# A gated pooling and forgetting-attention block: the transposes of V written to the score banks instead of the projection banks

## Chip, cores, metric

The kernel runs on one core of one Trainium2 chip. The metric is the device time of one execution in microseconds (us). Five engines work side by side, each through its own instructions in order: PE (TensorE, matmuls and transposes), ACT (ScalarE), DVE (VectorE), POOL (GpSimd) and SP (SyncE, which here issues transfers). They wait for one another by semaphores. PE's results go to PSUM, which this kernel uses as 8 banks of 128 x 512 fp32; a bank can be written again once everything in it has been read out ("evacuated") by ACT and DVE.

## What is computed

One decoder block on 1040 tokens (16 meta tokens, 1024 real ones) of width 1024. The part that matters here, cut from the reference:

```python
h = rmsnorm(x, norm_g)
proj = jnp.einsum('bld,dn->bln', h, w_in)
u_pool, z_pool, q, k, v, z_attn, f_logit, g_pool, g_attn = jnp.split(proj, _split_points(), axis=-1)
y_pool = causal_multiscale_pool(u_pool, pool_w, pool_scale) * jax.nn.silu(z_pool)
log_f = jax.nn.log_sigmoid((f_logit + b_forget).astype(jnp.float32))
y_attn = forgetting_attention(q, k, v, log_f).reshape(B, L, ATTN_WIDTH) * jax.nn.silu(z_attn)
merged = (jax.nn.sigmoid(g_pool) * jnp.einsum('blc,cd->bld', y_pool, w_up_pool)
          + jax.nn.sigmoid(g_attn) * jnp.einsum('blc,cd->bld', y_attn, w_up_attn))
return x + jnp.einsum('bld,de->ble', merged, w_out)
# in the attention, 8 heads of 64, causal, c = cumulative sum of log_f:
s = q @ k.T / 8 + c[query] - c[key];  o = softmax(s) @ v
```

## The kernel before

**Stages.** The norm, the transposes of the input and the projections of the first two heads come first (to about 55 us), then the attention (to about 466 us), then the gates, the up-projections and the output projection. Every product is done in fp32 precision by splitting operands into a high and a low part and adding three products (`g_mm3`): 24 matmuls per projection piece.

**Attention.** The 8 heads go in 4 pairs `p`. Each pair has 4 units (head `e` of the pair, half of the queries); the 16 units run one after the other. For a unit `qk` computes scores of one block of 128 keys against up to 512 queries (two matmuls, L691 and L692), ACT and DVE evacuate them (L696, L700). `soft` does the exponentials (L732 to L737) and `av` multiplies by V (L753). While unit i does `soft` and `av`, the scores of unit i+1 are computed.

**Filling.** PE's order is written out by the program, not by a scheduler. Between the attention's matmuls a queue (`Fill`, called through `F.pull`) hands out matmuls of the other projections in a set amount of PE time. Among them are `f_q`, `f_k` and `f_v` of the next pair: q, k and v of two heads. The orders of ACT, DVE and POOL come from a scheduler.

**V.** `f_v(p)` projects V with the channels on the partitions, in three pieces of 384, 384 and 272 tokens (`PIECES`). ACT copies each piece to `vt` in SBUF (L301). The attention needs V with the keys on the partitions, so `v_blocks` transposes `vt` in blocks of 128 keys on PE (L312) and ACT and DVE split the result into high and low part (L321, L322), for the two heads one after the other. After the second piece blocks 1 and 2 are transposed, after the third 3 to 5, and after another projection blocks 6 to 8 and 0. Pair 0 has its blocks 6 to 8 and 0 directly ahead of the first scores (L802).

**Banks.** In the attention the 8 PSUM banks are shared out so: `pj` two, for the projection pieces; `psS` two and `pk` one, which form a ring of three for the scores; `psT` two (running maxima and others); `psO` one (the output of `av`). The ring is turned by `third`: every third call gives the `pk` bank, which also carries the name `pj`, so in this kernel's profile a score in `pj` lies in the third bank of the ring. A projection piece takes a bank by `fill_bank`, which in the attention (`spare[0]` false) gives the two `pj` banks in turn; before the attention (`spare[0]` true) it turns through `pj` and `pk`.

Of the kernel before, what the change touches and what calls it, by code (L numbers as in the profile page):

```python
# [45 lines left out]
def r32(ap):  # L46
    return ap.bitcast(F32)
# [7 lines left out]
def tile_hybrid_block(ctx, tc, x, meta, norm_g, w_in, b_forget, pool_w, pool_scale,  # L55
# [118 lines left out]
    turn, spare = [0], [True]  # L174

    def third(pool, name):
        turn[0] += 1
        if turn[0] % 3 == 0:
            return pk.tile([128, 512], F32, name="pj")
        return pool.tile([128, 512], F32, name=name)  # L180

    def fill_bank():
        return third(pj, "pj") if spare[0] else pj.tile([128, 512], F32, name="pj")
# [121 lines left out]
            V[p, e] = ap_.tile([KB, NB, 2, 64], F32R, name="V", bufs=3)  # L305

    def v_blocks(p, *parts):
        pt = fill_bank().rearrange("p (n e d) -> p n e d", e=2, d=64)
        n = 0
        for b0, b1 in parts:  # L310
            for b in range(b0, b1):
                nc.tensor.transpose(pt[:, n], VT[p][:, KS[b]:KS[b] + KB], ident)  # L312
                n += 1
                yield 109.0
        for e in range(2):
            n = 0
            for b0, b1 in parts:
                pv = pt[:, n:n + b1 - b0]
                n += b1 - b0
                vh = V[p, e][:, b0:b1, e, :]  # L320
                nc.scalar.activation(vh, pv[:, :, e, :], AF.Copy)  # L321
                nc.vector.tensor_tensor(V[p, e][:, b0:b1, 1 - e, :], pv[:, :, e, :], r32(vh), op=ALU.subtract)  # L322
# [13 lines left out]
    def f_v(p):  # L336
        w = w_chunk(COL_V + p * 128)
        VT[p] = gp.tile([128, L], F32, name="vt", tag="g")
        v_alloc(p)
        for c0, c1 in PIECES:  # L340
            yield from v_piece(p, w, c0, c1)
            if c0:
                yield from v_blocks(p, {384: (1, 3), 768: (3, 6)}[c0])
# [135 lines left out]
    for n, (kind, t0, t1) in enumerate(todo):  # L479
# [29 lines left out]
        if n in (4, 7, 10):  # L509
            run(v_blocks(0, (max(1, 2 * (n // 3) - 2), 2 * (n // 3))))  # L510
    G_.close()
    spare[0] = False
    psS = P_.enter_context(tc.tile_pool(name="psS", bufs=2, space=PS, reuse_waits="tile"))
# [279 lines left out]
    def pair_fill(p):  # L793
        if p < 4:
            F.add(f"q{p}", f_q(p))
            F.add(f"k{p}", f_k(p), apart=True)
            F.add(f"v{p}", f_v(p), 4 * p - 2)
            F.add(f"v{p}", v_blocks(p, (6, 9), (0, 1)), 4 * p - 2, apart=True)
# [506 lines left out]
    for n in range(7):  # L1305
        if n < 6:
            prep(n + 1)
        ps = ba if n in (0, 2, 4, 6) else bb_
# [56 lines left out]
```

## Time and profile before

| what | value |
|---|---|
| three runs | 731.11, 730.85, 730.51 us; median 730.85 |
| profiled execution | 731.65 us, of which the span from first to last instruction 730.0 us |
| granted TensorE clock | 0.998 |
| PE busy | 714.1 us of the span |
| stalls of PE in the attention, 100 to 470 us | 5.8 us in four groups |

The profile is of one execution. `PE` rows are matmuls and transposes, `PEld` their weight loads, which run beside them. In a row of the timeline the first number is the start in us from the span's start, the second the time until the last of the row's instructions ended; `x4` is their count, and the bracket is the engine's idle time ahead of them and what ended it. Matmuls are pipelined: the end of one lies behind the start of the next, so what an instruction costs is read from start to start. In a row of the waits stand the total in us, the number of times and the longest. A stall of PE costs time only if nothing later would have waited anyway.

### The profile page before, as it was taken

The page shows a single profiled execution, that of the slowest core. Times are in us where ns is not written, and L with a number is a line of the kernel's source. Part 1 is how long each engine was busy: PE and PEld are TensorE (multiplying, and loading weights), DVE is VectorE, ACT ScalarE, POOL GpSimd, SP SyncE. Part 2 cuts the span into 40 slices and gives each one's busy share as a digit, 9 for nine tenths or more (in the row PEclk, how much of TensorE's full clock was granted, in tenths as well). Part 3 has the DMA queues.
Part 4 walks back from the last instruction along what each step waited for, and adds up shares of the span by engine and source line. Part 5 has one row for each costly group of instructions (what it writes and reads, how often), then busy time and mean ns, then how long its engine had stood idle before and what let it go on. Part 6 is the DMA issues. An engine that isn't in the chain of part 4 may idle for free.

```text
span 730.0 us, 10821 instructions
## 1 busy us (share of the span) xinstructions
PE 714.1 (98%) x3637; PEld 614.1 (84%) x3637; DVE 506.5 (69%) x913; ACT 425.0 (58%) x930; POOL 329.6 (45%) x409
## 2 busy tenths in 40 slices
PE   8999999999999989999999999999999999999996
PEld 6997999988889878789888888888888888888885
DVE  5743487676688766877876768765877654888775
ACT  6652577566686666667765577252766423525445
POOL 5412236638455574363643775493743010006142
PEclk9999999999999999999999999999999999999999
DMA  9201124772987558729556789486905367671006
GB/s 303 65 27 33 58 58 161 184 251 75 284 208 182 128 147 215 210 62 273 116 115 176 238 219 214 125 314 196 321 9 213 106 215 260 230 259 59 0 1 230
DMA packets 88505, 119.39 MB, mean 164 GB/s; under 512 B 11297, under 2 KB 54305, under 8 KB 86450
## 3 DMA queue, kind: packets, MB, share of 16 engines
q1 hardware_dynamic: 84896, 99.83, 42.4%
q0 software_dynamic: 2256, 16.25, 12.5%
q10 hardware_dynamic: 1298, 2.63, 1.0%
q8 instruction: 28, 0.46, 0.3%
q14 instruction: 27, 0.22, 0.1%
HBM read 92.81 MB, written 53.67 MB: 201 GB/s over the span
## 4 chain that ended last, share of the span: by engine, by line
PE 84%; ACT 5%; DVE 4%; issue 1%; POOL 0%; POOLq 0%; DVEq 0%; ACTq 0%
PE pj L171 52%; PE pj L1245 8%; PE pj L986 8%; PE po L753 5%; PE pt L986 3%; PE pt L1245 2%; PE ps L692 2%; PE ps L691 2%; ACT S L733 1%; PE pj L528 1%; PE pj L692 1%; PE pj L691 1%; ACT qa L269 1%; ACT ph L736 1%; DVE ql L273 0%
## 5 line engine op out<-in xcount | busy, mean ns | idle before, releaser
L171 PE MATMUL pj<-hh,whi 128*128 128x512 f32 (+3 forms) x640 | 146.0, 354 | 6.5 <-ACT vt L301 4.4
L171 PE MATMUL pj<-hh,wlo 128*128 128x512 f32 (+3 forms) x640 | 143.2, 350 | 0.3 <-POOL wlo L446 0.3
L171 PE MATMUL pj<-hl,whi 128*128 128x512 f32 (+3 forms) x640 | 141.5, 350 | 0.0
L171 PEld LDWEIGHTS pj<-hh,whi 128*128 128x128 f32 x640 | 107.7, 188 | 21.8 <-ACT vt L301 5.8
L159 POOL TENSOR_TENSOR wlo<-raw,whi 128x256 fp32r<-128x256 f32 x116 | 88.9, 809 | 79.2 <-ACT whi L157 26.9
L171 PEld LDWEIGHTS pj<-hl,whi 128*128 128x128 f32 x640 | 108.1, 188 | 12.0
L171 PEld LDWEIGHTS pj<-hh,wlo 128*128 128x128 f32 x640 | 107.9, 188 | 11.9 <-POOL wlo L446 0.5
L737 DVE TENSOR_TENSOR pl<-S,ph 128x512 fp32r<-128x512 f32 (+4 forms) x112 | 82.3, 743 | 25.7 <-ACT ph L736 24.6
L745 POOL TENSOR_TENSOR acc<-acc,S 128x272 f32<-128x272 f32 (+4 forms) x80 | 74.5, 931 | 13.8 <-ACT S L733 8.8
L705 DVE TENSOR_TENSOR pt<-pt,S 128x400 f32<-128x400 f32 (+2 forms) x96 | 46.6, 486 | 22.3 <-ACT S L696 20.1
L736 ACT ACTIVATE ph<-S 128x512 fp32r<-128x512 f32 (+4 forms) x112 | 52.9, 481 | 15.1 <-PE po L753 14.3
L137 POOL TENSOR_TENSOR gw<-graw,gw 128x256 fp32r<-128x256 f32 x40 | 45.8, 1180 | 29.6 <-ACT gw L966 13.1
L733 ACT ACTIVATE S<-S 128x512 f32<-128x512 f32 (+4 forms) x112 | 49.7, 478 | 10.8 <-DVE S L732 10.5
L732 DVE TENSOR_TENSOR S<-S,pt 128x512 f32<-128x512 f32 (+4 forms) x112 | 50.7, 497 | 0.7
L696 ACT ACTIVATE S<-ps,negc 128x512 f32<-128x512 f32 (+4 forms) x63 | 32.4, 518 | 20.8 <-PE ps L692 16.7
L986 PE MATMUL pj<-gh,gw 128*128 128x512 f32 x180 | 42.0, 389 | 0.0
L1138 DVE TENSOR_TENSOR rl<-pj,rl 128x512 f32<-128x512 f32 x32 | 22.0, 689 | 28.6 <-PE pj L171 28.2
L157 ACT ACTIVATE whi<-raw 128x512 fp32r<-128x512 f32 x58 | 34.4, 623 | 12.5 <-DMA raw<-in_w_in_dram 6.9
L986 PEld LDWEIGHTS pj<-gh,gw 128*128 128x128 f32 x180 | 33.8, 188 | 7.1
L743 POOL TENSOR_TENSOR acc<-S 128x400 f32<-128x400 f32 (+1 forms) x16 | 19.7, 1231 | 40.8 <-ACT S L733 40.8
L753 PE MATMUL po<-pl,V 128*128 128x512 f32 (+4 forms) x112 | 37.4, 334 | 0.0
L1245 PE MATMUL pj<-opw 128*128 128x512 f32 (+1 forms) x168 | 36.2, 374 | 0.0
(236 smaller groups left out, 1339.3 us busy)
## 6 DMA issues: line engine op xcount, KB each, us to landing
raw<-in_w_in_dram SPq DMA_DIRECT2D x31, 512.0 KB, 4.4
gs<-in_w_in_dram SPq DMA_DIRECT2D x5, 1024.0 KB, 10.0
td<-in_w_out_dram SPq DMA_DIRECT2D x5, 1024.0 KB, 8.2
xt<-in_x_dram SPq DMA_DIRECT2D x8, 512.0 KB, 7.5
sp_gp<-st SPq DMA_DIRECT2D x16, 256.0 KB, 4.1
gs<-gs POOLq DMA_DIRECT2D x4, 1024.0 KB, 9.0
td<-td POOLq DMA_DIRECT2D x4, 1024.0 KB, 9.2
sp_ga<-st SPq DMA_DIRECT2D x16, 256.0 KB, 5.2
```

What stands on the lines that cost most here:

```text
L137: ins = nc.gpsimd.tensor_tensor(out[:, c:c + 256], x[:, c:c + 256], y[:, c:c + 256], op=op)
L159: ins = nc.gpsimd.tensor_tensor(lo[:, k:k + 2], raw[:, k:k + 2], r32(hi[:, k:k + 2]), op=ALU.subtract)
L171: nc.tensor.matmul(ps, a, b, start=(i == 0), stop=(i == len(seq) - 1))
L705: nc.vector.tensor_tensor(m[:kb, c0:], m[:kb, c0:], s[:kb, c0:], op=ALU.max)
L732: nc.vector.tensor_tensor(s[:kb, c0:], s[:kb, c0:], self.pm[:kb, c0:], op=ALU.subtract)
L733: exps.append(nc.scalar.activation(s[:kb, c0:], s[:kb, c0:], AF.Exp))
L736: nc.scalar.activation(ph[:kb, c0:], s[:kb, c0:], AF.Copy)
L737: dves.append(nc.vector.tensor_tensor(pl[:kb, c0:], s[:kb, c0:], r32(ph[:kb, c0:]), op=ALU.subtract))
L745: accs.append(nc.gpsimd.tensor_tensor(acc[:kb, c0:], acc[:kb, c0:], s[:kb, c0:], op=ALU.add))
L753: nc.tensor.matmul(self.po[:, c0:], v, r[:kb, c0:], start=(b == 0 and i == 0), stop=(b == self.nb - 1 and i == 1))
L986: nc.tensor.matmul(ps, op_w[n][p][k // 2][:, k % 2, i * 128:(i + 1) * 128], op_h[n][q][k // 2][:, k % 2], start=start and m == 0, stop=m = ...
L1245: nc.tensor.matmul(ps, pick(A_, k, p)[:, i * 128:(i + 1) * 128], pick(B_, k, q)[:, c0:c1], start=start and n == 0, stop=n == 11, skip_grou ...
```

## The change

The transposes of V in the attention take their bank from the ring of the scores (`third(psS, "ps")`) instead of from the two `pj` banks. Before the attention nothing changes.

```diff
     def v_blocks(p, *parts):
-        pt = fill_bank().rearrange("p (n e d) -> p n e d", e=2, d=64)
+        pt = (fill_bank() if spare[0] else third(psS, "ps")).rearrange("p (n e d) -> p n e d", e=2, d=64)
```

Ten calls of `v_blocks` lie in the attention: one of pair 0, three each of pairs 1, 2 and 3. No instruction comes or goes, and PE and SP keep their order; each call turns the ring by one, so the later scores lie in other banks of it, and the projection pieces alternate between their two banks without the transposes in between.

First place, PE in `f_v(1)`: the end of the second piece (`pj_1904`), the transposes of blocks 1 and 2 (`pj_1969`), and the first matmuls of the third piece (`pj_1976`). Before:

```order
L171 MATMUL pj_1904<-hh1_124,wlo_1833 128x384 x4
L312 MATMUL pj_1969<-ident_96,vt_1840 128x128 [waits Activation_49]
L312 MATMUL pj_1969<-ident_96,vt_1840 128x128
L171 MATMUL pj_1976<-hh0_122,whi_1832 128x272 [waits Activation_49]
L171 MATMUL pj_1976<-hh0_122,whi_1832 128x272 x3
```

The same place with the change:

```order
L171 MATMUL pj_1904<-hh1_124,wlo_1833 128x384 x4
L312 MATMUL pj_1969<-ident_96,vt_1840 128x128 [waits DVE_49]
L312 MATMUL pj_1969<-ident_96,vt_1840 128x128
L171 MATMUL pj_1976<-hh0_122,whi_1832 128x272 x4
L171 MATMUL pj_1976<-hh1_124,whi_1832 128x272
```

The third piece had the bank of the second and waited for ACT, which copies the second piece to `vt`; now it has the bank of the first and carries no wait, and the transposes (here in the `pk` bank, hence still `pj`) wait for DVE, which reads an earlier score.

Second place, PE a little later: the end of the third piece, the transposes of blocks 3 to 5 (2028), and the first matmuls of the next projection (`pj_2047`). Before:

```order
L171 MATMUL pj_1976<-hh1_124,wlo_1833 128x272 x4
L312 MATMUL pj_2028<-ident_96,vt_1840 128x128 [waits DVE_49,PE_49]
L312 MATMUL pj_2028<-ident_96,vt_1840 128x128 x2
L171 MATMUL pj_2047<-hh0_122,whi_2038 128x512 [waits PE_49,Activation_49]
L171 MATMUL pj_2047<-hh0_122,whi_2038 128x512 x3
```

With the change:

```order
L171 MATMUL pj_1976<-hh1_124,wlo_1833 128x272 x4
L312 MATMUL ps_2028<-ident_96,vt_1840 128x128 [waits DVE_49,Activation_49]
L312 MATMUL ps_2028<-ident_96,vt_1840 128x128 x2
L171 MATMUL pj_2047<-hh0_122,whi_2038 128x512 x4
L171 MATMUL pj_2047<-hh1_124,whi_2038 128x512 x4
```

Here too the projection behind the transposes loses its wait.

Third place, PE at the first unit: the transposes of pair 0 (1040) and the first five scores, of 512, 400, 272, 144 and 16 queries, among matmuls of a projection. Before:

```order
L312 MATMUL pj_1040<-ident_96,vt_283 128x128 x3
L691 MATMUL ps_1055<-qa_228,ka_160 128x512
L692 MATMUL ps_1055<-ql_229,ka_160 128x512
L171 MATMUL pj_1064<-hh0_122,whi_965 128x272 [waits Activation_49]
L171 MATMUL pj_1064<-hh0_122,whi_965 128x272 x3
L691 MATMUL ps_1069<-qa_228,ka_160 128x400
L692 MATMUL ps_1069<-ql_229,ka_160 128x400
L171 MATMUL pj_1064<-hh1_124,whi_965 128x272 x4
L691 MATMUL pj_1080<-qa_228,ka_160 128x272
L692 MATMUL pj_1080<-ql_229,ka_160 128x272
L171 MATMUL pj_1064<-hl0_123,whi_965 128x272 x4
L691 MATMUL ps_1090<-qa_228,ka_160 128x144 [waits DVE_49]
```

With the change:

```order
L312 MATMUL ps_1040<-ident_96,vt_283 128x128 x4
L691 MATMUL ps_1055<-qa_228,ka_160 128x512
L692 MATMUL ps_1055<-ql_229,ka_160 128x512
L171 MATMUL pj_1064<-hh0_122,whi_965 128x272 [waits Activation_49]
L171 MATMUL pj_1064<-hh0_122,whi_965 128x272 x3
L691 MATMUL pj_1069<-qa_228,ka_160 128x400
L692 MATMUL pj_1069<-ql_229,ka_160 128x400
L171 MATMUL pj_1064<-hh1_124,whi_965 128x272 x4
L691 MATMUL ps_1080<-qa_228,ka_160 128x272 [waits DVE_49]
L692 MATMUL ps_1080<-ql_229,ka_160 128x272
L171 MATMUL pj_1064<-hl0_123,whi_965 128x272 x4
L691 MATMUL ps_1090<-qa_228,ka_160 128x144 [waits DVE_49]
```

By the built program's memory map the third score (1080) now lies in the bank of the first (1055), and the fourth (1090) in the bank of the transposes (1040); before, the third had the `pk` bank and the fourth the bank of the first. So the fourth score now waits for the last of the eight instructions that evacuate the transposes.

On ACT, DVE and POOL the scheduler moves a few rows by a few places near 93, 162, 264 and 357 us: exponentials, evacuations of keys and V, and some of the weight splits (L157, L159).

## Prediction

> **What bounds the kernel now.** I read the page first: the busy shares and the chain that ended last.
>
> ```profile
> PE 714.1 (98%) x3637; PEld 614.1 (84%) x3637; DVE 506.5 (69%) x913; ACT 425.0 (58%) x930; POOL 329.6 (45%) x409
> PE 84%; ACT 5%; DVE 4%; issue 1%; POOL 0%; POOLq 0%; DVEq 0%; ACTq 0%
> ```
>
> PE is busy for 714.1 of 730.0 us and carries 84% of the chain; no other engine comes near. What ends the kernel sooner must take away PE's idle time, some 16 us in all, or PE's work, which this change leaves as it is. So the next view is the busy time by stretches, to see where the idle time of the attention lies.
>
> ```profile
> 180.00:275.00 95.00, 92.75 (x476) 80.88 (x475) 70.84 (x146) 64.41 (x160) 53.80 (x66) 1.00 0.73 190
> 370.00:466.00 96.00, 95.93 (x451) 80.28 (x450) 72.10 (x137) 59.25 (x142) 58.58 (x68) 1.00 0.74 192
> 466.00:600.00 134.00, 134.00 (x592) 110.66 (x590) 91.11 (x97) 66.72 (x88) 54.44 (x51) 1.00 0.59 194
> ```
>
> The first column behind the length is PE. Where pair 2 of V is prepared (180 to 275) it idles 2.25 us; after the last preparation (370 to 466), with the same attention work, 0.07 us, and from 466 to 600 nothing. The attention's chain through DVE and ACT therefore does not hold PE up. What does is in the waits of PE from 100 to 470 us:
>
> ```profile
> PE pj L171 <- ACT vt L301: 4.4, 6, 1.0
> PE pj L171 <- ACT qa L269: 0.8, 1, 0.8
> PE pj L171 <- DVE ka L296: 0.4, 1, 0.4
> PE pj L171 <- ACT st L354: 0.2, 1, 0.2
> ```
>
> Projections (L171) wait for the evacuation of an earlier projection. Six of the waits, 4.4 us, are for the copy of V into `vt`: two in each of three pairs. No row has `po`: the multiplication by V never waits for the softmax, nor do the scores for their banks.
>
> **The nine waits that go.** In the attention a projection's transposes take one `pj` bank, so the projection behind them gets the bank of the projection just ahead of them, whose copy has hardly begun. With the change the projections alternate among themselves, and each finds a bank whose copy was started a whole piece earlier. The timeline of PE shows the nine places, each as the transposes and the first matmuls behind:
>
> ```profile
> 157.36 0.38 PE L312 MATMUL pj<-ident,vt 128*128 128x128 f32 x2
> 158.70 0.89 PE L171 MATMUL pj<-hh,whi 128*128 128x272 f32 x5 [0.96 <-ACT vt L301]
> ...
> 162.06 0.49 PE L312 MATMUL pj<-ident,vt 128*128 128x128 f32 x3
> 162.77 2.14 PE L171 MATMUL pj<-hh,whi 128*128 128x512 f32 x8 [0.22 <-ACT vt L301]
> ...
> 176.81 0.60 PE L312 MATMUL pj<-ident,vt 128*128 128x128 f32 x4
> 177.66 0.50 PE L171 MATMUL pj<-hh,whi 128*128 128x512 f32 x1 [0.25 <-ACT st L354]
> ...
> 258.91 0.38 PE L312 MATMUL pj<-ident,vt 128*128 128x128 f32 x2
> 260.20 1.14 PE L171 MATMUL pj<-hh,whi 128*128 128x272 f32 x7 [0.91 <-ACT vt L301]
> ...
> 264.23 0.49 PE L312 MATMUL pj<-ident,vt 128*128 128x128 f32 x3
> 265.69 1.20 PE L171 MATMUL pj<-hh,whi 128*128 128x512 f32 x4 [0.96 <-ACT vt L301]
> ...
> 280.72 0.66 PE L312 MATMUL pj<-ident,vt 128*128 128x128 f32 x4
> 281.44 2.12 PE L171 MATMUL pj<-hh,whi 128*128 128x512 f32 x8
> ...
> 350.01 0.38 PE L312 MATMUL pj<-ident,vt 128*128 128x128 f32 x2
> 350.96 1.27 PE L171 MATMUL pj<-hh,whi 128*128 128x272 f32 x8 [0.57 <-ACT vt L301]
> ...
> 354.07 0.49 PE L312 MATMUL pj<-ident,vt 128*128 128x128 f32 x3
> 355.29 2.11 PE L171 MATMUL pj<-hh,whi 128*128 128x512 f32 x8 [0.72 <-ACT vt L301]
> ...
> 369.77 0.60 PE L312 MATMUL pj<-ident,vt 128*128 128x128 f32 x4
> 370.13 0.31 PE L691 MATMUL ps<-qa,ka 128*128 128x144 f32 x1
> 370.28 0.28 PE L692 MATMUL ps<-ql,ka 128*128 128x144 f32 x1
> 370.62 0.50 PE L171 MATMUL pj<-hh,whi 128*128 128x512 f32 x1
> ```
>
> The bracket understates the loss, since the pipeline also runs empty while the last transposes end. From start to start it is the whole distance less what unhindered transposes take. Four take 0.36 us (369.77 to 370.13, where a score follows at once); two take 0.14 us, by a place ahead of the attention:
>
> ```profile
> 42.70 0.38 PE L312 MATMUL pj<-ident,vt 128*128 128x128 f32 x2
> 42.84 0.36 PE L171 MATMUL pj<-hh,whi 128*128 128x256 f32 x1
> ```
>
> Three I put between, at 0.25 us. Pair 1 loses 1.34 - 0.14 = 1.20, 0.71 - 0.25 = 0.46 and 0.85 - 0.36 = 0.49; pair 2 loses 1.15, 1.21 and 0.36; pair 3 loses 0.81, 0.97 and, behind the 144-wide score at 370.28 that takes some 0.11 us, 0.23. Together 6.9 us. The least is what the waits list names, 4.4 + 0.2 = 4.6 us. I take 6.9, since 370 to 466 shows that PE without such waits runs without gaps.
>
> Does it stay gained? Behind each place PE's next waits must hold too. The transposes themselves now wait for a score's evacuation; the score tile of three turns ago was written several us earlier, and its readers are done long before (no score waits for a bank in the list above). The remaining chain moves along: the softmax of a unit starts with PE's own scores.
>
> **The wait that comes.** Pair 0's transposes are directly followed by the five scores of the first unit with little other work between, and the fourth score stands behind the evacuation of the transposes. Rows of PE, then of DVE:
>
> ```profile
> 85.69 0.29 PE L691 MATMUL pj<-qa,ka 128*128 128x272 f32 x1
> ...
> 86.44 0.23 PE L691 MATMUL ps<-qa,ka 128*128 128x144 f32 x1
> 86.50 0.28 PE L692 MATMUL ps<-ql,ka 128*128 128x144 f32 x1
> 86.61 0.33 PE L171 MATMUL pj<-hl,whi 128*128 128x272 f32 x1
> ...
> 85.16 0.34 DVE L700 SCALAR_TENSOR_TENSOR S<-ps,negc,mask 128x112 f32<-128x112 f32 x1 [0.39 <-ACT S L696]
> 87.11 0.21 DVE L322 TENSOR_TENSOR V<-pj,V 128x64 fp32r<-128x64 f32 x1
> ```
>
> The last evacuation ended at 87.32 us; the order of ACT and DVE up to it is unchanged. The score started at 86.44. With some 0.1 us for the hand-over it starts at 87.4: PE stands 1.0 us, with the projection queued behind. The third score, now in the first one's bank, waits for a DVE row that ended at 85.16 + 0.34 = 85.50, ahead of its start at 85.69: about nothing. The softmax of the unit moves by less than PE, since only its last two scores are late, so part of the 0.4 us that PE stood for `ka` soon after is used up. I take 1.0 - 0.3 = 0.7 us; the ends are 0.4 (all of the 0.4 and some more comes back) and 1.5 (the last scores delay the whole first softmax by the full stall and half as much again).
>
> **At the other nine places the ring costs nothing**, I think, because the next use of the transposes' bank is three turns away. The tightest is pair 2's last group, by the rows of DVE and PE:
>
> ```profile
> 286.48 0.21 DVE L322 TENSOR_TENSOR V<-pj,V 128x64 fp32r<-128x64 f32 x1
> ...
> 289.34 0.40 PE L691 MATMUL ps<-qa,ka 128*128 128x512 f32 x1
> ```
>
> The bank of the transposes was read out at 286.48 + 0.21 = 286.69 us and by the new order would be needed at 289.34: 2.65 us of cover. If it were gone each group would cost like the first.
>
> **Moved rows.** The weight splits that the scheduler puts a few places later feed projections far off: the one at 357.67 us is read by PE in the next projection, at 370.62.
>
> ```profile
> 357.67 0.62 ACT L157 ACTIVATE whi<-raw 128x512 fp32r<-128x512 f32 x1
> ```
>
> Three rows of some 0.6 us behind it would still leave over 10 us. Cost zero, with this as its cover. SP's order is untouched and no transfer moves on its queue; each follows its trigger, earlier by what PE gains.
>
> **Sum.** 6.9 - 0.7 = 6.2 us off the profiled execution: 731.65 - 6.2 = 725.45 (its span 730.0 would be 723.8). The execution lies 0.8 us above the median of the runs, 730.85, so the runs come to 724.65, say 724.7.
>
> [...]
>
> **Rivals.**
>
> 1. The gain is partly given back. PE comes up to 6 us earlier to work of DVE, ACT, POOL and the transfers, and where one of them is not led by PE, it waits there. For it: DVE is busy 72.10 of 96 us at the end of the attention, and the wait for `qa`, 0.8 us, shows ACT late once already. Against it: PE idles 0.07 us in those 96. Half the gain: 730.85 - 3.1 = 727.8.
> 2. Slower: the evacuation of V blocks the ring at every group, not only the first. Price 1.0 us each, ten times: 10 - 6.9 = 3.1 us lost, 734.0. It decides from 0.69 us per group. For it: the stall at 86.44. Against it: the 2.65 us of cover at the tightest other place.
> 3. No change: another limit stands right behind the bank, such as the weights or the softmax, and PE waits for it instead. 730.85. Against it: PE shows no such wait where V is not prepared.
>
> **How the numbers follow.** Forecast 724.7 with 75%, partly given back 15%, no change 6%, slower 4%. Within 0.2% (1.5 us) this measurement can't tell a change. So faster 0.90, same 0.06, slower 0.04. The range: at the low end 6.9 - 0.4 and 0.9 for runs and the references taken, 723.5; at the high end the given-back case, 727.5, where a gain of 4.6 less a wait of 1.3 would also lie.
>
> **What would show it.** In the waits of PE the row `<- ACT vt L301` is gone; the windows around the preparations show PE idle by some 0.6 us where they had 2; a new row has scores (L691) waiting for DVE `V` (L322) once, about 1.0 us. PE's busy time stays near 714. The attention ends some 6 us earlier and everything after keeps its length. It is wrong if `V` appears there many times, or `po` waits for `pl`, or the stretch behind the attention grows.

## The result, and the profile after

| | before | with the change |
|---|---|---|
| median of the runs | 730.98 us (730.51 to 731.36, 4 runs) | 724.42 us (724.02 to 725.24, 4 runs) |
| ratio | | 0.9912, 95% interval 0.9895 to 0.9929 |
| profiled execution, its span | 731.65, 730.0 us | 724.48, 722.8 us |

The change takes 6.56 us off; 6.2 us were forecast (724.7 us). The page of the profile after, busy shares and the chain that ended last:

```profile
PE 711.7 (98%) x3637; PEld 614.8 (85%) x3637; DVE 507.9 (70%) x913; ACT 424.0 (59%) x930; POOL 329.9 (46%) x409
PE 88%; DVE 3%; ACT 2%; issue 1%; POOLq 0%; POOL 0%; ACTq 0%; DVEq 0%
```

PE still bounds the kernel, and more so: its part of the chain rises from 84% to 88%, while ACT's falls from 5% to 2%. PE's work is the same 3637 matmuls. The prediction had PE's busy time stay near 714 us, and it fell by 2.4 us: before, the ends of matmuls that ran out into a gap counted as busy (the two transposes at 157.36 us with 0.38 us, where from start to start two take 0.13 to 0.14). The numbers below fit that, since from 110 to 466 us the starts gain 7.14 us and the idle time only 4.74. The waits of PE from 20 to 470 us, after:

```profile
PE ps L691 <- DVE V L322: 0.8, 1, 0.8
PE pj L171 <- ACT qa L269: 0.8, 1, 0.8
PE pt L233 <- DVE hl L236: 0.5, 1, 0.5
PE pj L171 <- DVE ka L296: 0.4, 1, 0.4
```

The rows for `vt` (4.4 us) and `st` (0.2 us) are gone. One row is new: a score waits once for the evacuation of V. The row for `pt` was there before as well. The busy time of the same stretch, before and then after (the first number behind the length is PE):

```profile
110.00:466.00 356.00, 350.12 (x1800) 306.03 (x1800) 261.82 (x528) 235.59 (x582) 203.62 (x241) 1.00 0.68 180
110.00:466.00 356.00, 354.86 (x1831) 311.64 (x1830) 267.45 (x533) 235.55 (x583) 204.84 (x241) 1.00 0.69 183
```

PE idled 5.88 us there and idles 1.14 us now, and 31 more matmuls fit in. The timeline of PE after, at the first two places of pair 1, and then the first of pair 2:

```profile
157.33 0.38 PE L312 MATMUL pj<-ident,vt 128*128 128x128 f32 x2
157.46 0.87 PE L171 MATMUL pj<-hh,whi 128*128 128x272 f32 x5
...
160.77 0.49 PE L312 MATMUL ps<-ident,vt 128*128 128x128 f32 x3
161.01 1.17 PE L171 MATMUL pj<-hh,whi 128*128 128x512 f32 x4
...
256.58 0.38 PE L312 MATMUL ps<-ident,vt 128*128 128x128 f32 x2
256.71 1.12 PE L171 MATMUL pj<-hh,whi 128*128 128x272 f32 x7
```

From the transposes to the next projection there are 0.13 and 0.24 us now, where there were 1.34, 0.71 and 1.29. And the place that the change made worse, PE and then DVE:

```profile
86.78 0.34 PE L691 MATMUL ps<-qa,ka 128*128 128x144 f32 x1 [0.78 <-DVE V L322]
...
86.51 0.21 DVE L322 TENSOR_TENSOR V<-ps,V 128x64 fp32r<-128x64 f32 x1
```

The last evacuation of V ends at 86.51 + 0.21 = 86.72 us, and the fourth score starts 0.06 us later.

Since PE's order is the same in both kernels, each matmul's start can be set against its own start before. The differences, in us (negative is earlier), here and for the experiments below; the column heads are times in the profile before:

| kernel | 83 | 110 | 157 | 180 | 300 | 375 | end | from 83 to the end |
|---|---|---|---|---|---|---|---|---|
| the change | -0.59 | -0.03 | -0.03 | -2.31 | -5.03 | -7.17 | -7.17 | -6.58 |
| the same, repeated | -0.92 | -0.37 | -0.37 | -2.65 | -5.35 | -7.47 | -7.47 | -6.55 |
| pair 0 back in a projection bank | -0.42 | -0.39 | -0.39 | -2.66 | -5.37 | -7.47 | -7.47 | -7.05 |
| pair 0 alone in the ring | -0.39 | +0.15 | +0.16 | +0.13 | +0.14 | +0.11 | +0.11 | +0.50 |
| third bank with the projections | -1.16 | -0.64 | +0.90 | -1.38 | -4.18 | -7.34 | -6.54 | -5.38 |
| changed kernel, copies doubled | -1.13 | -0.58 | -0.58 | -2.86 | -5.53 | -7.67 | -7.67 | -6.54 |
| kernel before, copies doubled | -0.87 | -0.86 | -0.86 | +2.70 | +4.16 | +5.61 | +5.60 | +6.47 |

### The profile page after: what moved, and what is told of

It is laid out like the page before. It is cut to its first block, busy times and chain, and to the rows that moved or that the text cites. A ratio compares the mean times of both kernels' runs of the same rounds, so it can differ in the third digit from the quotient of the medians.

```text
span 722.8 us, 10818 instructions
## 1 busy us (share of the span) xinstructions
PE 711.7 (98%) x3637; PEld 614.8 (85%) x3637; DVE 507.9 (70%) x913; ACT 424.0 (59%) x930; POOL 329.9 (46%) x409
## 4 chain that ended last, share of the span: by engine, by line
PE 88%; DVE 3%; ACT 2%; issue 1%; POOLq 0%; POOL 0%; ACTq 0%; DVEq 0%
PE pj L171 55%; PE pj L1245 8%; PE pj L986 8%; PE po L753 5%; PE pt L986 3%; PE pt L1245 2%; PE ps L692 2%; PE ps L691 2%; PE pj L528 1%; PE pj L692 1%; PE pj L691 1%; ACT qa L269 1%; DVE ql L273 0%; PE ps L312 0%; ACT S L733 0%
## 5 line engine op out<-in xcount | busy, mean ns | idle before, releaser
L159 POOL TENSOR_TENSOR wlo<-raw,whi 128x256 fp32r<-128x256 f32 x116 | 89.7, 817 | 88.3 <-ACT whi L157 38.0
L737 DVE TENSOR_TENSOR pl<-S,ph 128x512 fp32r<-128x512 f32 (+4 forms) x112 | 84.2, 761 | 24.9 <-ACT ph L736 24.1
L696 ACT ACTIVATE S<-ps,negc 128x400 f32<-128x400 f32 (+4 forms) x65 | 33.6, 518 | 19.5 <-PE ps L692 18.7
L157 ACT ACTIVATE whi<-raw 128x512 fp32r<-128x512 f32 x58 | 34.4, 624 | 11.4 <-DMA raw<-in_w_in_dram 6.1
L753 PE MATMUL po<-ph,V 128*128 128x512 f32 (+4 forms) x112 | 36.0, 321 | 0.0
```

The costliest lines, as they stand in the source:

```text
L159: ins = nc.gpsimd.tensor_tensor(lo[:, k:k + 2], raw[:, k:k + 2], r32(hi[:, k:k + 2]), op=ALU.subtract)
L737: dves.append(nc.vector.tensor_tensor(pl[:kb, c0:], s[:kb, c0:], r32(ph[:kb, c0:]), op=ALU.subtract))
L753: nc.tensor.matmul(self.po[:, c0:], v, r[:kb, c0:], start=(b == 0 and i == 0), stop=(b == self.nb - 1 and i == 1))
```

## The experiments

**The changed kernel once more.** No edit.

> The changed kernel once more, as the mark for the others. The first two heads' start lay 0.6 us earlier in the profile after than before, in a stretch (up to 83 us) where both kernels have the same code in the same order. If that is chance, as I hold, the span here differs from 722.8 us by some tenths either way and the shift of PE between 83 us and the end is again some 6.6 us. If the change did it, the start is 0.6 us early again. Time 724.4, 0.988 to 0.993 of before.

Measured: 724.19 us, ratio to before (731.12) 0.9908, interval 0.9893 to 0.9924. From 83 us on, PE gained 6.55 us, as in the first profile (6.58). The first 83 us are where profiles of the same code differ: the seven kernels of the table lie 0.39 to 1.16 us ahead of the profile before, those without a gain too, and the repeat of the doubled copies further down lies 0.01 us ahead. So that part varies from one execution to the next and is not the change's.

**Pair 0's transposes back in a projection bank.** The part of the change that cost something is taken back (the line removed is the changed kernel's).

```diff
-        pt = (fill_bank() if spare[0] else third(psS, "ps"))...
+        pt = (third(psS, "ps") if p and not spare[0] else fill_bank())...
```

> Only pair 0's group of transposes goes back to a projection bank; the nine groups of pairs 1 to 3 stay in the ring. Theory (nine bank waits removed, one added at the first unit, partly paid back by waits that were there anyway): the stall of the fourth score (0.95 us) is gone, but the waits for ka (0.39) and near 102.7 us (0.13) are back, so 0.4 us less than the changed kernel: 724.0. Rival A (the new stall delays the first softmax and through it everything): 0.95 us or more less, 723.5 or lower. Rival B (the stall costs nothing, since the attention makes it up): no difference, 724.4. In the trace the theory wants PE at 110 us to lie 0.4 us earlier against the time at 83 us.

Measured: 723.59 us, ratio 0.9899, interval 0.9885 to 0.9912; the runs range from 723.55 to 724.18, those of the changed kernel beside it from 724.03 to 725.07. The stall at the first unit is gone and a wait for the keys is back. The waits of PE and its timeline here:

```profile
PE pj L171 <- DVE ka L296: 0.6, 2, 0.4
...
97.61 0.49 PE L171 MATMUL pj<-hh,whi 128*128 128x272 f32 x2 [0.22 <-DVE ka L296]
```

In the table the difference from 83 to 110 us is +0.03 in place of +0.56 and +0.55, so some 0.5 us of the whole: near the theory's 0.4, and neither the full 0.95 us nor nothing, as the rivals had it. The time alone doesn't decide between the theory (724.0) and rival A (723.5 or lower); the trace does. This version has the lowest median of all that ran.

**Pair 0's transposes alone in the ring** (again set against the changed kernel's line).

```diff
-        pt = (fill_bank() if spare[0] else third(psS, "ps"))...
+        pt = (fill_bank() if spare[0] or p else third(psS, "ps"))...
```

> Only pair 0's group goes to the ring; pairs 1 to 3 write a projection bank as before. Theory: the bad part of the change alone. The stall of about 0.95 us, less 0.5 us that PE would have waited soon after: 0.4 us slower than before, 731.4, and the six waits for vt (4.4 us) all there. Rival (the gain came from another order of ACT and DVE at the first unit, or from the turned ring as such, not from the projections' banks): a good part of the 6.6 us shows here, 725 to 729.

Measured: 731.37 us against 731.12, ratio 1.0002, interval 0.9993 to 1.0011. The time alone can't tell +0.4 us from none; the rival's 725 to 729 it excludes. The waits show both parts of the theory:

```profile
PE pj L171 <- ACT vt L301: 4.3, 6, 1.0
...
PE ps L691 <- DVE V L322: 0.8, 1, 0.8
```

The stall is there without the gain, and in the table PE loses 0.54 us from 83 to 110 us and nothing after. A turned ring as such brings nothing.

**The third bank with the projections.** In the kernel before, projections and transposes turn through three banks, scores through two.

```diff
 def fill_bank():
-        return third(pj, "pj") if spare[0] else pj.tile([128, 512], F32, name="pj")
+        return third(pj, "pj")
...
-            ps = third(psS, "ps")
+            ps = psS.tile([128, 512], F32, name="ps")
```

> The third bank goes to the other side: projections and transposes turn through three banks (two pj and pk), the scores through two only. Theory: a third piece finds the bank of the first, so the nine waits go here too, without the ring (7 us). What is new is that each score waits for the evacuation of the one two turns before, which shows what the ring's cover is worth: at the narrow ends of the units (144 and 16 queries) two turns are only 1 to 2 us, and the cover of three turns was 1.4 to 1.7 us there, so 0.3 to 1 us is lost in most of the 16 units: 5 to 14 us. Together 729 to 738, best guess 732, with a new row of scores (L691) waiting for DVE S (L700) or ACT S (L696). Rival (two score banks are enough, so that the ring has slack to spare): 724.

Measured: 724.90 us, ratio 0.9916, interval 0.9902 to 0.9930. Half of the expectation failed. The nine waits are gone here too, without the ring, so it is the distance between the projections' uses of a bank that counts. But two banks for the scores cost far less than I said. The waits of PE, and the place of the longest:

```profile
PE ps L691 <- ACT S L696: 1.7, 4, 0.6
PE ps L691 <- DVE S L700: 0.8, 1, 0.8
...
86.56 0.25 PE L691 MATMUL ps<-qa,ka 128*128 128x16 f32 x1 [0.78 <-DVE S L700]
```

Five waits of 2.5 us (3.8 us from start to start), one at the narrow end of the first unit and four ahead of 512-wide scores, none at the narrow ends of the other units, where I had put most of them. My error there was to take a whole turn of 1 to 2 us off the cover. The kernel before shows the actual cover of two turns at such an end, DVE and then PE:

```profile
392.66 0.34 DVE L700 SCALAR_TENSOR_TENSOR S<-pj,negc,mask 128x128 f32<-128x128 f32 x1
...
393.52 0.17 PE L691 MATMUL ps<-qa,ka 128*128 128x16 f32 x1
```

The score of two turns ago was read out at 393.00, 0.52 us ahead of the last one. On the other side this kernel gains some 0.6 us at 234 us and 1.0 us at 309 us, where projections of keys and queries had waited for their banks; the rows for `qa` and `ka` are gone from its list.

**Copies doubled, kernel before.** ACT writes each copy of V into `vt` twice for pairs 1 to 3, with the same values.

```diff
-            nc.scalar.activation(VT[p][:, d], ps[:, c], AF.Copy)
+            for _ in range(2 if p else 1):
+                nc.scalar.activation(VT[p][:, d], ps[:, c], AF.Copy)
```

> The kernel before, with every copy of V into vt of pairs 1 to 3 written twice by ACT (the same values again), so that a projection piece's bank comes free later by one copy: 0.38 us for the second pieces, some 0.34 us for the third. Theory (PE stands at six places for that copy): the six waits for vt grow by 0.34 to 0.38 us each, 2.2 us in all, 4.4 to 6.6 in the list; 733.0. Rival (the waits are not on the path, something else ends later): no more than 0.5 us, 731.

Measured: 736.68 us against 730.95, ratio 1.0076, interval 1.0059 to 1.0093. The copies are on the path, but the size was off: 5.7 us, not 2.2. PE's waits, then the first stall on PE, then the three ACT rows ahead of it:

```profile
PE pj L171 <- ACT vt L302: 9.4, 6, 2.1
...
158.79 1.37 PE L171 MATMUL pj<-hh,whi 128*128 128x272 f32 x5 [1.92 <-ACT vt L302]
...
157.70 0.49 ACT L302 ACTIVATE vt<-pj 128x384 f32<-128x384 f32 x1
158.09 0.27 ACT L322 ACTIVATE V<-pj 128x128 fp32r<-128x128 f32 x1
158.24 0.50 ACT L302 ACTIVATE vt<-pj 128x384 f32<-128x384 f32 x1
```

The waits grew by 5.0 us, since the scheduler set other ACT instructions between the two copies (here an evacuation of V, in the third pieces also exponentials, their high parts or weight splits). The rest of the 6.47 us that this profile lost from 83 us on, some 1.5 us, is the granted clock behind this stall. Busy times and, third from the end, the clock, behind the stall of 1.92 us and behind one of 2.05 us in pair 2:

```profile
158.80:162.10 3.30, 3.30 (x15) 3.30 (x16) 2.60 (x6) 1.92 (x4) 0.00 (x0) 0.53 0.05 13
...
269.80:272.00 2.20, 2.16 (x9) 1.80 (x10) 0.39 (x2) 0.84 (x2) 2.20 (x4) 1.00 0.00 0
```

**Copies doubled, changed kernel.** The same edit on the changed kernel.

> The changed kernel with the same doubled copies. Theory: the copy is no longer waited for, the transposes behind it start a piece later (3.4 us), so the doubling is hidden: within 0.4 us of the changed kernel, 724.4, and no row of PE waiting for vt. Rival (ACT sets the time in these stretches, 12 more copies of about 0.36 us delay it): 4 us more than the changed kernel, 728.

Measured: 723.98 us, ratio to before (730.95) 0.9905, interval 0.9891 to 0.9920; from 83 us on 6.54 us gained, against 6.55 to 6.58 without the doubling. The same 12 copies that cost 5.7 us there cost nothing here. This pair of runs is the direct evidence that PE waited for the copy, that it does so no longer, and that ACT has room for it.

**The doubled copies once more, kernel before,** to see whether the clock's drop repeats. No further edit.

> The kernel before with doubled copies of V once more. The first run lost 5.7 us instead of 2.2: 5.0 us more of waits for vt (9.4 against 4.4), and some 1.5 us because the granted clock was 0.50 from 159 to 161 us and 0.65 from 161 to 163, behind a stall of 1.92 us; behind another stall of 2.05 us it stayed 1.00. If the drop hangs on the stall, it is there again at the same place. If it is chance, the waits are 9.4 us again and the clock is 1.00 there, and the time is 1.5 us less, 735.

Measured: 737.38 us, ratio 1.0074, interval 1.0056 to 1.0092; waits for `vt` 9.1 us. In the profile the drop is there again in the same piece, after a stall of 1.60 us:

```profile
159.38 0.90 PE L171 MATMUL pj<-hh,whi 128*128 128x272 f32 x5 [1.60 <-ACT vt L302]
...
160.60:163.80 3.20, 3.20 (x16) 3.20 (x15) 2.67 (x5) 2.62 (x5) 0.93 (x1) 0.50 0.40 85
```

Whether the drop came in every execution is not shown. Of the four runs of the first trial two have a mean granted clock of 0.996 and took 737.25 and 737.15 us, two have 0.998 and took 736.20 and 736.12; the 3.20 us at half clock in the row above are 0.002 of the mean. Only the first of these was profiled, so for the others this is a guess.

**Copies tripled, kernel before.** `range(3 if p else 1)`.

> The same with three copies. Theory (PE stands for the copy): the waits for vt grow again, by 2 to 5 us, to 11 to 14 us, 738 to 742, as the second copy added 5.0. If a longer stall halves the clock, the granted clock falls behind more of the six places, up to 1.5 us each on top; if not, it is 1.00 behind all of them.

Measured: 745.75 us, ratio 1.0193, interval 1.0176 to 1.0210, some 4 us above the 738 to 742 that I gave for the waits alone. The waits grew to 13.7 us, inside the expected range; the rest fits the halved clock behind three of the six places, for which I had allowed up to 1.5 us each. PE's waits, and the three stretches in which it was halved:

```profile
PE pj L171 <- ACT vt L302: 13.7, 6, 2.5
...
165.40:169.00 3.60, 3.60 (x9) 2.90 (x10) 0.89 (x4) 3.02 (x8) 3.44 (x3) 0.53 0.00 0
...
360.00:363.40 3.40, 3.40 (x18) 3.40 (x17) 3.25 (x5) 2.71 (x6) 2.61 (x2) 0.51 0.83 193
...
366.90:370.30 3.40, 3.38 (x8) 2.71 (x9) 0.28 (x1) 1.64 (x5) 3.32 (x5) 0.52 0.02 5
```

## Why the prediction held

**The nine waits.** Set out as 1.20, 0.46, 0.49 for pair 1, 1.15, 1.21, 0.36 for pair 2 and 0.81, 0.97, 0.23 for pair 3, together 6.9 us; the steps in PE's starts between the two profiles are 1.19, 0.52, 0.54; 1.20, 1.18, 0.33; 0.85, 0.98, 0.26: together 7.05. Reading the loss from start to start, rather than from the waits list (4.6), was what made the sum right. The 0.25 us put in for three transposes measured 0.24. That it is the bank that was waited for, and not the path by chance, the doubled copies show.

**The wait that came.** Forecast 1.0 us at the fourth score of the first unit. That score moved by 0.94 us against the matmuls ahead of it and the next matmul by another 0.11, together 1.05. The some 0.1 us in it for the hand-over had no row behind it; measured were 0.06 us (86.72 to 86.78). The prediction then let 0.3 us come back at the 0.4 us that PE stood for `ka` "soon after", and here it misread the list. That wait stands at 234.5 us, in the preparation of pair 2, and nothing came back there. What came back lay at another wait for `ka`, of 0.23 us at 98.03 us, outside the list, which began at 100 us. Both places, before and then after:

```profile
98.03 0.49 PE L171 MATMUL pj<-hh,whi 128*128 128x272 f32 x2 [0.23 <-DVE ka L296]
...
234.52 0.70 PE L171 MATMUL pj<-hh,whi 128*128 128x512 f32 x2 [0.37 <-DVE ka L296]
...
98.11 0.41 PE L171 MATMUL pj<-hh,whi 128*128 128x272 f32 x2
...
232.19 0.70 PE L171 MATMUL pj<-hh,whi 128*128 128x512 f32 x2 [0.37 <-DVE ka L296]
```

From start to start 0.47 us came back at 98 us and 0.06 at 102.7, so the net is some 0.55 us against the 0.7 of the sum. The principle held, that a later wait of PE takes up part of a new one; that its size came near was luck, since the wait it was priced from had no part in it. Taking pair 0 back to a projection bank is worth that 0.5 us.

**Cover at the other places.** The ring costs nothing at the nine others: the list has one row for V, with one wait. The experiment with two score banks shows that the cover was larger than I believed.

**The rivals.** Partly given back (727.8 by its own sum, where the range names the same case at 727.5): from 375 us to the end no matmul moves against another by 0.01 us, so nothing of the gain is lost behind the attention; the softmax, the transfers and POOL came along. The ring blocked at every group, and no change: excluded by the waits and by the interval.

**The weight splits and other moved rows**, costed at nothing, show in no wait.

## What to carry to other kernels

A short side job (here transposes) that shares two accumulators with a stream of long ones throws off their alternation: the long job behind it gets the bank that is just being read out (7.05 us at nine places here). Give the side job a bank from a pool that turns slowly, and look for the one place where that pool turns fast, since the new wait appears there (0.78 us at the first unit here). Read a stall's cost from start to start (7.05 us here, 4.6 in the waits list), and before pricing a new wait, see which later waits of the same engine will shrink by it, and at what time they stand (0.47 us came back at 98 us here).

## What I had not expected of the hardware

A short stall of PE cost more than its length here, though not every time. With the copies doubled, stalls of 1.92 and 1.60 us in one place were followed by 3.30 and 3.20 us at a granted clock of 0.53 and 0.50, which cost about another 1.5 to 1.6 us (3.30 times 0.47, 3.20 times 0.50). With the copies tripled this came behind three stalls of six, with 3.40 to 3.60 us at 0.51 to 0.53; PE's row for the second of them:

```profile
359.48 1.82 PE L171 MATMUL pj<-hh,whi 128*128 128x272 f32 x8 [2.52 <-ACT vt L302]
```

But behind a stall of 2.05 us in the first doubled run, and behind one of 2.12 us in the first place of the tripled run, the clock stayed at 1.00. The stretches behind these two:

```profile
269.80:272.00 2.20, 2.16 (x9) 1.80 (x10) 0.39 (x2) 0.84 (x2) 2.20 (x4) 1.00 0.00 0
272.00:274.00 2.00, 2.00 (x11) 1.69 (x10) 1.27 (x2) 0.54 (x2) 2.00 (x3) 1.00 0.00 0
...
158.00:162.00 4.00, 2.96 (x23) 2.96 (x24) 3.95 (x9) 3.67 (x9) 0.12 (x1) 1.00 0.11 22
```

So the length of a stall alone does not tell these cases apart: the clock fell behind 1.60 us and not behind 2.05. What does was not shown. In the profiles before and after, every stretch of 4 us from the start to 720 us has a clock of 1.00, so the clock has no part in the 6.6 us between these two.
